# Places for the scaled q, k, v sums, and the order of the output gate's products, in a two-layer hybrid encoder

## The chip, the cores and the metric

One core of a Trainium2 chip runs the whole program. The metric is the device time of one execution in microseconds (us). The kernel before takes 1235.73 us, the median of three runs (1235.57 to 1237.52).

## What is computed

The reference is an encoder of two layers over 256 positions of width 1024, all in float32. Each layer adds half a SwiGLU block (inner width 2816), then a mixer, then half of another SwiGLU block; a norm stands ahead of each. The change lies in the mixer:

```
gq, gk, gv, gz, gb, ga, c_q, c_kv, k_rope, gate_logits = split_cols(h @ w_in[l])
qkv = silu(conv5(concat(gq, gk, gv)))        # depthwise, centred, 5 taps over the positions
qh, kh = l2norm of the 4 heads of q and of k;  vh = the 4 heads of v
o = gated delta rule forwards + backwards (chunks of 64, with a triangular solve)
y_a = (rmsnorm(o) * silu(gz)) @ gdn_proj     # gz: the output gate
y_b = 8 heads of softmax attention from the latents c_q, c_kv @ mla_proj
x = x + (sigmoid(g_A) * y_a + sigmoid(g_B) * y_b) @ w_out
```

q, k and v are 512 columns wide each, so the convolution has 1536 channels.

## The kernel before

**Products.** Every product is made of three: the activations and the weights are both split into a high part in the type fp32r and the rest, and high x high, high x low and low x high are added in PSUM. `weights` (L118) loads a block of weights with a DMA on SP's queue into `raw`, copies it on ScalarE into `whi` (L130) and subtracts on VectorE into `wlo` (L131). `mm3` issues the three products (L148 to L150). `dense_t` runs over the inner dimension for two accumulators, one per half of the 256 positions, and calls an evacuation for each. The accumulators `acc` are three PSUM tiles; two more rings are `ms` (3) and `gd` (2).

**The mixer.** The projection with `w_in` is done in pieces. `qkv_group(grp)` (L546) makes 256 of the 1536 channels, with the channels on the partitions: groups 0 and 1 are q, 2 and 3 are k, 4 and 5 are v. Its 48 products (L557) fill one `acc` tile. VectorE scales that by the norm's factor of each position into `pre` (L565), a tile of 2 x 260 elements per partition whose two elements at either end GpSimd sets to zero (L563, L564). Then, for each of the two halves of the channels, five taps are added up in `cv` on VectorE, the first as a product (L571) and four as multiply-add (L573). ScalarE makes `th`, the tanh of `cv` (L577), and VectorE finishes SiLU into `qkT` or, for v, into a part of `ysb` (L578). `pre`, `cv` and `th` have one place each, so every group waits for the one before it, and `lengths` (L581), which sums the squares of four heads (GpSimd L586, then TensorE L590), uses `cv` as well.

Other steps that are met below: `mla_dense` (L618) makes q, k and v of four attention heads from the latents, with the weights `mla_w_ukv` and then `mla_w_uq`; `mla_heads` (L642) transposes q and k of these heads on TensorE (L651), copies them out on ScalarE (L654), and returns the attention of the heads, which is run later. `gdn_decay` (L734) makes the decay matrices with products on GpSimd (L743, L755). `gdn_la` (L758) multiplies q and k (TensorE L763, VectorE L767). `gdn_base` (L780) inverts triangular blocks of 16 in fifteen serial steps on GpSimd (L805, L807) with VectorE before and after (L810), and `inv0` (L835) and the following put the blocks together on TensorE (L839 and on). `gate` (L985) makes the merge gates into tiles of the tag `gate`, which has six places. `ev_z` (L980) evacuates the output gate.

**What sets the order.** The program is written as one sequence, L1007 to L1081, and built under a planner (L1114): each instruction has a place in the sequence as its priority, and the planner runs a simulated clock and gives each engine, whenever it is free, the ready instruction that comes first. `tc.high_priority(offset=n)` lets instructions rank as if they stood n places earlier. The order that comes out is fixed: on the chip each engine works through its own queue in that order and stands still when the instruction at its head must wait. A tile can be taken only when a place of its tag is free. The part of the sequence around the change is

```
qkv_group(2); the beta, decay and q-latent columns; qkv_group(3); qkv_group(0); the kv-latent columns
gdn_scalars(); gdn_decay(0); lengths(4); latent(cq); qkv_group(1); gdn_decay(1); latent(ckv)
gdn_coeffs(); gdn_la(1); gdn_la(0); m0 = mla_dense(0); at0 = mla_heads(*m0)
gdn_base() at priority; dense(..., C_Z, ...), the output gate; inv_zero(); inv0(0) and on
mla_dense(1); two merge gates; ...; qkv_group(4); qkv_group(5); ...
```

Of the kernel before, what the change touches and what calls it, by code (L numbers as in the profile page):

```python
# [16 lines left out]
ALU = mybir.AluOpType  # L17
# [3 lines left out]
P = 128  # L21
D = 1024
S = 256
NT = 2
NKC = D // P
# [8 lines left out]
C_Z, C_BA, C_KV, C_G = 1536, 2048, 2448, 2736  # L34
# [3 lines left out]
def encoder_trunk(ctx: ExitStack, tc: tile.TileContext, x, positions, norm_ffn1, ffn1_w_gate, ffn1_w_up,  # L38
# [4 lines left out]
    V, A, G, T = nc.vector, nc.scalar, nc.gpsimd, nc.tensor  # L43
# [57 lines left out]
    xh = pitched(main, NKC, "xh")  # L101
    xl = pitched(main, NKC, "xl")
# [71 lines left out]
    def dense(ah, al, nk, src, c0, w, evac, **kw):  # L174
        dense_t([(ah[:, k], al[:, k]) for k in range(nk)], src, c0, w, evac, **kw)
# [249 lines left out]
    def mixer(l, next_gain):  # L425
# [3 lines left out]
        wl_ = w_in[l]  # L429
# [3 lines left out]
        with tc.tile_pool(name="mix", bufs=1) as mp:  # L433
            def t2(tag, bufs, shape=(P, NH, P)):
                return mp.tile(list(shape), F32, tag=tag, name=tag, bufs=bufs)
# [17 lines left out]
            rb = mp.tile([P, S], F32, name="rb")  # L453
# [92 lines left out]
            def qkv_group(grp):  # L546

                ps = acc()
                pc = ps.rearrange("p (c s) -> p c s", c=2)
                ws = weights(wl_[:, grp * 256:(grp + 1) * 256], NKC, 256)  # L550

                for c in range(2):
                    cc = slice(c * P, (c + 1) * P)
                    terms = [m for kc, (wh, wlo) in enumerate(ws)
                             for m in ((wh, xh[:, kc]), (wh, xl[:, kc]), (wlo, xh[:, kc]))]
                    for i, (w, a) in enumerate(terms[::-1] if c else terms):
                        T.matmul(pc[:, c].rearrange("p (t s) -> p t s", s=P), lhsT=w[:, cc], rhs=a, start=(i == 0),  # L557
                                 stop=(i == len(terms) - 1))
                if grp >= 4:
                    vT[grp - 4] = ysb[0][:, (grp - 4) * 512:(grp - 3) * 512].rearrange("p (c s) -> p c s", s=S)  # L560
                pre = t2("pre", 1, (P, 2, S + 4))
                cv = t2("cv", 1, (P, 2, S))
                G.memset(pre[:, :, 0:2], 0.0)  # L563
                G.memset(pre[:, :, S + 2:S + 4], 0.0)  # L564
                V.tensor_tensor(out=pre[:, :, 2:S + 2], in0=pc, in1=rb[:, None, :].to_broadcast([P, 2, S]), op=ALU.mult)  # L565
                for c in range(2):
                    ch = grp * 2 + c
                    for d in range(5):
                        wc = ccol[:, l * 60 + d * 12 + ch:l * 60 + d * 12 + ch + 1]
                        if d == 0:  # L570
                            V.tensor_scalar(out=cv[:, c], in0=pre[:, c, 0:S], scalar1=wc, scalar2=None, op0=ALU.mult)  # L571
                        else:
                            V.scalar_tensor_tensor(out=cv[:, c], in0=pre[:, c, d:d + S], scalar=wc, in1=cv[:, c],  # L573
                                                   op0=ALU.mult, op1=ALU.add)

                th = t2("th", 1, (P, 2, S))
                A.activation(out=th, in_=cv, func=AF.Tanh, scale=0.5)  # L577
                V.scalar_tensor_tensor(out=qkT[:, grp * 2:grp * 2 + 2, :] if grp < 4 else vT[grp - 4], in0=th, scalar=1.0,  # L578
                                       in1=cv, op0=ALU.add, op1=ALU.mult)

            def lengths(c0):  # L581

                pss = gdp()[:, :4 * NT * 32].rearrange("p (c t s) -> p c t s", c=4, t=NT)
                for c in (0, 2):
                    sq = t2("cv", 1, (P, 2, S))
                    G.tensor_tensor(out=sq, in0=qkT[:, c0 + c:c0 + c + 2, :], in1=qkT[:, c0 + c:c0 + c + 2, :], op=ALU.mult)  # L586
                    sv = sq.rearrange("p c (t g s) -> p g c t s", t=NT, g=4)
                    for g in range(4):

                        T.matmul(pss[g * 32:(g + 1) * 32, c:c + 2], lhsT=ones, rhs=sv[:, g], start=True, stop=True)  # L590
                rows = t2("rows", 1, (P, 2, 4 * NT * 32))
                A.copy(out=rows[:, 0], in_=pss.rearrange("p c t s -> p (c t s)"))
                V.transpose(out=rows[:, 1], in_=rows[:, 0])
                V.tensor_scalar(out=ssq[:, :, c0:c0 + 4],
                                in0=rows[:, 1].rearrange("p (c t s) -> p t c s", c=4, t=NT)[:, :, :, 0],
                                scalar1=4.0 * EPS, scalar2=None, op0=ALU.add)
                for t in range(NT):
                    G.tensor_tensor(out=rqk[:, t, c0:c0 + 4], in0=ssq[:, t, c0:c0 + 4], in1=neghalf[:, :4], op=ALU.pow)
# [422 lines left out]
            gdn_la(1)  # L1021
            gdn_la(0)
            m0 = mla_dense(0)
            at0 = mla_heads(*m0)
            with tc.high_priority(offset=2000):
                gdn_base()
            dense(xh, xl, NKC, wl_, C_Z, 512, ev_z)
            inv_zero()
            with tc.high_priority(offset=2000):
                inv0(0)  # L1030
# [88 lines left out]
```

## Time and profile before

| what | value |
|---|---|
| runs, median (lowest to highest) | 1235.73 us (1235.57 to 1237.52) |
| the profiled execution, its time | 1238.92 us |
| the profiled execution, its span | 1237.2 us |
| mean granted TensorE clock | 0.985 of full speed |
| TensorE busy | 1204.2 us, 97% |
| VectorE busy | 770.9 us, 62% |
| ScalarE busy | 622.4 us, 50% |
| GpSimd busy | 132.3 us, 11% |
| mean DMA rate | 164 GB/s |

The span is from the first to the last instruction; the execution's time has 1.72 us more. In the profile PE is TensorE's products, PEld its weight loads, DVE is VectorE, ACT ScalarE, POOL GpSimd, SP the queue that issues the DMAs of the weights. L12 is line 12 of the kernel. An instruction is written as its line, its operation, what it writes and reads by the program's tile names, and its shape; x4 says that a line stands for four instructions in a row. In square brackets is the time for which the engine had been idle before it, and the work that ended that idle time. The granted clock (PEclk) is TensorE's, as a share of 2.4 GHz: 1.00 is that, 0.50 is 1.2 GHz, and a value between them is a stretch with some of both. The two mixers lie at 196 to 432 us and at 807 to 1043 us.

### The profile page before, as it was taken

How to read it: one execution, taken by the hardware profiler on the slowest of the kernel's cores; microseconds unless marked ns; L12 is line 12 of the kernel's file. 1: busy time of each engine (PE TensorE's matmuls, PEld its weight loads, DVE VectorE, ACT ScalarE, POOL GpSimd, SP SyncE). 2: the span in 40 equal slices, each digit the busy share in tenths (PEclk: the TensorE clock that was granted, in tenths of full speed). 3: DMA queues.
4: the chain of work that ended last, by engine and by line, in shares of the span. 5: the costliest groups of instructions: out<-in, count | busy, mean ns of one | idle time of the engine just before them, and what ended most of it. 6: DMA issues, size and time to landing. Idle time of an engine off the chain costs nothing.

```text
span 1237.2 us, 17605 instructions
## 1 busy us (share of the span) xinstructions
PE 1204.2 (97%) x7064; PEld 1016.9 (82%) x7064; DVE 770.9 (62%) x1125; ACT 622.4 (50%) x911; POOL 132.3 (11%) x238
## 2 busy tenths in 40 slices
PE   9999999899999999999999999997999999999997
PEld 6888889778778888888888888897778888888886
DVE  5665556986857665554555554588858676555554
ACT  6554445547455454444454453465455455544443
POOL 1000001454101000000000000015540000000010
PEclk9999999989899999999999999998998999999999
DMA  7564555445222555556555556553453135565552
GB/s 265 181 197 144 201 188 179 139 125 174 94 88 103 171 185 189 176 173 207 187 178 187 186 170 194 182 158 122 124 168 104 69 138 186 178 198 180 191 187 85
DMA packets 114576, 202.70 MB, mean 164 GB/s; under 512 B 4107, under 2 KB 30399, under 8 KB 114495
## 3 DMA queue, kind: packets, MB, share of 16 engines
q1 hardware_dynamic: 114031, 200.52, 49.9%
q8 instruction: 55, 0.90, 0.3%
q10 hardware_dynamic: 464, 1.06, 0.2%
q14 instruction: 26, 0.21, 0.1%
HBM read 200.52 MB, written 1.05 MB: 163 GB/s over the span
## 4 chain that ended last, share of the span: by engine, by line
PE 87%; DVE 5%; POOL 4%; ACT 2%; issue 2%; DMA 0%; POOLq 0%; SPq 0%; ACTq 0%
PE acc L148 24%; PE acc L149 24%; PE acc L150 24%; PE acc L557 4%; PE ms L198 2%; DVE wlo L131 2%; POOL t L807 1%; PE ms L665 1%; POOL bt L805 1%; PE gd L148 1%; PE gd L149 1%; PE gd L150 1%; PE gd L938 1%; DVE cv L573 1%; PE gd L763 1%
## 5 line engine op out<-in xcount | busy, mean ns | idle before, releaser
L131 DVE TENSOR_TENSOR wlo<-raw,whi 128x1024 fp32r<-128x1024 f32 (+3 forms) x388 | 470.4, 1215 | 368.4 <-ACT whi L130 365.9
L130 ACT CAST whi<-raw 128x1024 fp32r<-128x1024 f32 (+3 forms) x388 | 399.3, 1033 | 424.0 <-PE acc L150 384.1
L149 PE MATMUL acc<-wlo,xh 128*128 128x512 f32 (+3 forms) x968 | 360.6, 374 | 0.0
L150 PE MATMUL acc<-whi,xl 128*128 128x512 f32 (+3 forms) x968 | 357.4, 372 | 0.0
L148 PE MATMUL acc<-whi,xh 128*128 128x512 f32 (+3 forms) x968 | 344.8, 376 | 0.1
L149 PEld LDWEIGHTS acc<-wlo,xh 128*128 128x128 f32 x968 | 182.4, 188 | 29.5 <-issue 0.4
L148 PEld LDWEIGHTS acc<-whi,xh 128*128 128x128 f32 x968 | 181.5, 189 | 30.3 <-ACT xh L115 0.8
L150 PEld LDWEIGHTS acc<-whi,xl 128*128 128x128 f32 x968 | 182.1, 188 | 29.3
L149 PE MATMUL acc<-wlo,hh 128*128 128x512 f32 x352 | 137.4, 390 | 0.0
L150 PE MATMUL acc<-whi,hl 128*128 128x512 f32 x352 | 137.1, 390 | 0.0
L148 PE MATMUL acc<-whi,hh 128*128 128x512 f32 x352 | 127.3, 392 | 0.0
L150 PEld LDWEIGHTS acc<-whi,hl 128*128 128x128 f32 x352 | 66.1, 188 | 13.8
L148 PEld LDWEIGHTS acc<-whi,hh 128*128 128x128 f32 x352 | 66.1, 188 | 13.7
L149 PEld LDWEIGHTS acc<-wlo,hh 128*128 128x128 f32 x352 | 66.1, 188 | 13.3
L148 PE MATMUL acc<-whi,fr 128*128 128x512 f32 (+1 forms) x152 | 60.3, 403 | 9.1 <-DVE pre L565 7.9
L149 PE MATMUL acc<-wlo,fr 128*128 128x512 f32 (+1 forms) x152 | 59.9, 396 | 0.0
L150 PE MATMUL acc<-whi,fr 128*128 128x512 f32 (+1 forms) x152 | 57.5, 395 | 2.4 <-DVE fr L116 2.4
L557 PE MATMUL acc<-xl,whi 128*128 128x256 f32 x192 | 55.3, 288 | 0.0
L557 PE MATMUL acc<-xh,wlo 128*128 128x256 f32 x192 | 54.2, 292 | 1.0 <-DVE wlo L131 1.0
L557 PE MATMUL acc<-xh,whi 128*128 128x256 f32 x192 | 54.9, 289 | 0.0
L573 DVE SCALAR_TENSOR_TENSOR cv<-pre,ccol,cv 128x256 f32<-128x256 f32 x96 | 51.5, 569 | 0.1
L563 POOL MEMSET pre<- 128x4 f32 x12 | 1.2, 104 | 425.3 <-PE acc L150 341.0
(298 smaller groups left out, 1271.9 us busy)
## 6 DMA issues: line engine op xcount, KB each, us to landing
raw<-in_ffn_w_up_dram SPq DMA_DIRECT2D x40, 1024.0 KB, 5.1
raw<-in_ffn_w_down_dram SPq DMA_DIRECT2D x40, 1024.0 KB, 4.9
raw<-in_ffn_w_gate_dram SPq DMA_DIRECT2D x38, 1024.0 KB, 5.0
raw<-in_w_in_dram SPq DMA_DIRECT2D x32, 1024.0 KB, 5.0
raw<-in_w_out_dram SPq DMA_DIRECT2D x8, 1024.0 KB, 4.9
raw<-in_ffn_w_gate_dram SPq DMA_DIRECT2D x12, 512.0 KB, 3.7
raw<-in_ffn_w_up_dram SPq DMA_DIRECT2D x8, 512.0 KB, 3.7
raw<-in_ffn_w_down_dram SPq DMA_DIRECT2D x8, 512.0 KB, 3.3
```

The lines of the kernel that those rows point to most:

```text
L130: A.copy(out=hi[:, :n * w], in_=raw[:, k0 * w:(k0 + n) * w])
L131: V.tensor_tensor(out=lo[:, :n * w], in0=raw[:, k0 * w:(k0 + n) * w], in1=hi[:, :n * w].bitcast(F32), op=ALU.subtract)
L148: T.matmul(ps[t][:, :n], lhsT=a1, rhs=w[0], start=start, stop=False)
L149: T.matmul(ps[t][:, :n], lhsT=a1, rhs=w[1], start=False, stop=False)
L150: T.matmul(ps[t][:, :n], lhsT=a2, rhs=w[0], start=False, stop=stop)
L198: T.transpose(out=pt[:, i * S + t * P:i * S + (t + 1) * P], in_=srcs[t][:, (j + i) * P:(j + i + 1) * P], identity=ident)
L557: T.matmul(pc[:, c].rearrange("p (t s) -> p t s", s=P), lhsT=w[:, cc], rhs=a, start=(i == 0), stop=(i == len(terms) - 1))
L573: V.scalar_tensor_tensor(out=cv[:, c], in0=pre[:, c, d:d + S], scalar=wc, in1=cv[:, c], op0=ALU.mult, op1=ALU.add)
L665: T.matmul(sc[:, t * S:(t + 1) * S], lhsT=qT[:, t * P:(t + 1) * P], rhs=kT, start=True, stop=True)
L763: T.matmul(pa[:, (h - hp) * 256:(h - hp + 1) * 256], lhsT=qkT[:, 4 + h, t * P:(t + 1) * P], rhs=qkT[:, h:h + 5:4, t * P:(t + 1) * P], star ...
L805: G.tensor_tensor(out=tv, in0=M[:, b + 1:16, b:b + 1].to_broadcast([P, na, nb]), in1=Y[:, b:b + 1, 0:nb].to_broadcast([P, na, nb]), op=ALU ...
L807: G.tensor_tensor(out=Y[:, b + 1:16, 0:nb], in0=Y[:, b + 1:16, 0:nb], in1=tv, op=ALU.add)
```

## The change

In `qkv_group`, the scaled sums of groups 0 to 3 are put into the tag `gate` (six places, before used by the merge gates alone), and `pre` remains for groups 4 and 5, without the zeroed ends: the memsets are gone, and each tap at an edge covers fewer positions, with the centre tap first. `cv` has two places instead of one. The scaling gets a priority of 150 places. The tanh is written over the scaled sums, and the tag `th` is gone. In the mixer's sequence, the output gate's products are moved ahead of `mla_heads` of the first four heads, which holds the transposes.

```diff
@@ -558,22 +558,23 @@
                                  stop=(i == len(terms) - 1))
                 if grp >= 4:
                     vT[grp - 4] = ysb[0][:, (grp - 4) * 512:(grp - 3) * 512].rearrange("p (c s) -> p c s", s=S)
-                pre = t2("pre", 1, (P, 2, S + 4))
-                cv = t2("cv", 1, (P, 2, S))
-                G.memset(pre[:, :, 0:2], 0.0)
-                G.memset(pre[:, :, S + 2:S + 4], 0.0)
-                V.tensor_tensor(out=pre[:, :, 2:S + 2], in0=pc, in1=rb[:, None, :].to_broadcast([P, 2, S]), op=ALU.mult)
+
+                pre = t2("gate", 6, (P, 2, S)) if grp < 4 else t2("pre", 1, (P, 2, S))
+                cv = t2("cv", 2, (P, 2, S))
+                with tc.high_priority(offset=150):
+                    V.tensor_tensor(out=pre, in0=pc, in1=rb[:, None, :].to_broadcast([P, 2, S]), op=ALU.mult)
                 for c in range(2):
                     ch = grp * 2 + c
-                    for d in range(5):
+                    for d in (2, 0, 1, 3, 4):
                         wc = ccol[:, l * 60 + d * 12 + ch:l * 60 + d * 12 + ch + 1]
-                        if d == 0:
-                            V.tensor_scalar(out=cv[:, c], in0=pre[:, c, 0:S], scalar1=wc, scalar2=None, op0=ALU.mult)
+                        if d == 2:
+                            V.tensor_scalar(out=cv[:, c], in0=pre[:, c], scalar1=wc, scalar2=None, op0=ALU.mult)
                         else:
-                            V.scalar_tensor_tensor(out=cv[:, c], in0=pre[:, c, d:d + S], scalar=wc, in1=cv[:, c],
+                            o, i = (slice(2 - d, S), slice(0, S + d - 2)) if d < 2 else (slice(0, S + 2 - d), slice(d - 2, S))
+                            V.scalar_tensor_tensor(out=cv[:, c, o], in0=pre[:, c, i], scalar=wc, in1=cv[:, c, o],
                                                    op0=ALU.mult, op1=ALU.add)
 
-                th = t2("th", 1, (P, 2, S))
+                th = pre
                 A.activation(out=th, in_=cv, func=AF.Tanh, scale=0.5)
                 V.scalar_tensor_tensor(out=qkT[:, grp * 2:grp * 2 + 2, :] if grp < 4 else vT[grp - 4], in0=th, scalar=1.0,
                                        in1=cv, op0=ALU.add, op1=ALU.mult)
@@ -582,7 +583,7 @@
 
                 pss = gdp()[:, :4 * NT * 32].rearrange("p (c t s) -> p c t s", c=4, t=NT)
                 for c in (0, 2):
-                    sq = t2("cv", 1, (P, 2, S))
+                    sq = t2("cv", 2, (P, 2, S))
                     G.tensor_tensor(out=sq, in0=qkT[:, c0 + c:c0 + c + 2, :], in1=qkT[:, c0 + c:c0 + c + 2, :], op=ALU.mult)
                     sv = sq.rearrange("p c (t g s) -> p g c t s", t=NT, g=4)
                     for g in range(4):
@@ -1021,10 +1022,10 @@
             gdn_la(1)
             gdn_la(0)
             m0 = mla_dense(0)
+            dense(xh, xl, NKC, wl_, C_Z, 512, ev_z)
             at0 = mla_heads(*m0)
             with tc.high_priority(offset=2000):
                 gdn_base()
-            dense(xh, xl, NKC, wl_, C_Z, 512, ev_z)
             inv_zero()
             with tc.high_priority(offset=2000):
                 inv0(0)
```

## Rows read from the trace of the kernel before

**Rows 1.** The page: the span, and busy time of each engine with its share.

```profile
span 1237.2 us, 17605 instructions
...
PE 1204.2 (97%) x7064; PEld 1016.9 (82%) x7064; DVE 770.9 (62%) x1125; ACT 622.4 (50%) x911; POOL 132.3 (11%) x238
```

**Rows 2.** Stretches of 10 us: stretch, its length, busy time of each engine, PEclk, DMA.

```profile
220.00:230.00 10.00, 10.00 (x81) 10.00 (x80) 9.32 (x26) 6.05 (x10) 0.14 (x2) 1.00 0.57 167
230.00:240.00 10.00, 8.90 (x67) 8.24 (x66) 9.88 (x16) 5.64 (x14) 8.16 (x7) 1.00 0.58 186
240.00:250.00 10.00, 4.86 (x18) 3.77 (x17) 10.00 (x14) 4.12 (x9) 6.23 (x8) 0.77 0.36 130
```

**Rows 3.** TensorE's waits over the whole span: total us, times, longest us.

```profile
PE acc L148 <- DVE pre L565: 7.9, 2, 3.9
...
PE gd L839 <- DVE XC L816: 3.4, 2, 1.7
...
PE ms L651 <- ACT qk L654: 2.8, 2, 1.4
```

**Rows 4.** Timeline of TensorE: start us, us, instruction, idle before and its releaser.

```profile
224.38 0.28 PE L557 MATMUL acc<-xh,whi 128*128 128x256 f32 x1
...
239.41 0.28 PE L557 MATMUL acc<-xh,whi 128*128 128x256 f32 x1
...
247.87 0.66 PE L148 MATMUL acc<-whi,fr 128*128 128x384 f32 x1 [3.94 <-DVE pre L565]
...
266.37 1.47 PE L651 MATMUL ms<-ident,m 128*96 128x128 f32 x12
...
268.38 0.40 PE L150 MATMUL acc<-whi,xl 128*128 128x512 f32 x1
...
271.57 0.64 PE L651 MATMUL ms<-ident,m 128*96 128x128 f32 x4 [1.40 <-ACT qk L654]
...
272.42 1.78 PE L763 MATMUL gd<-qkT 128*128 128x256 f32 x4 [0.21 <-DVE qkT L578]
...
317.29 1.07 PE L839 MATMUL gd<-XC,LA 32*32 32x32 f32 x64 [1.71 <-DVE XC L816]
...
318.94 1.09 PE L682 MATMUL ms<-ident,pr 128*128 128x128 f32 x4 [0.58 <-DVE pr L677]
```

**Rows 5.** Three stretches after TensorE's gaps, columns as in rows 2.

```profile
247.90:254.00 6.10, 6.10 (x28) 5.59 (x29) 2.72 (x5) 2.84 (x5) 1.04 (x1) 0.64 0.26 86
272.40:278.00 5.60, 5.58 (x18) 4.55 (x19) 5.60 (x14) 1.92 (x5) 0.00 (x0) 0.70 0.34 89
317.30:325.00 7.70, 7.12 (x117) 6.31 (x120) 7.17 (x15) 3.06 (x7) 0.00 (x0) 0.57 0.39 132
```

**Rows 6.** Timeline of VectorE in the convolutions of groups 0 and 1.

```profile
229.96 0.68 DVE L565 TENSOR_TENSOR pre<-acc,rb 128x512 f32<-128x512 f32 x1
...
243.85 2.01 DVE L131 TENSOR_TENSOR wlo<-raw,whi 128x768 fp32r<-128x768 f32 x1
...
247.04 0.68 DVE L565 TENSOR_TENSOR pre<-acc,rb 128x512 f32<-128x512 f32 x1
```

**Rows 7.** VectorE's instructions on tile cv alone: stretch, length, busy (count), PEclk, DMA.

```profile
205.00:215.00 10.00, 4.02 (x10) 1.00 0.62 185
233.00:247.00 14.00, 8.52 (x10) 0.94 0.46 151
```

**Rows 8.** Timeline of ScalarE about the first attention heads' copies.

```profile
269.84 0.63 ACT L577 ACTIVATE th<-cv 128x512 f32<-128x512 f32 x1 [4.93 <-DVE cv L573]
...
270.94 1.54 ACT L654 COPY qk<-ms 96x512 f32<-96x512 f32 x3
```

**Rows 9.** Timeline of GpSimd: the squares of the k heads.

```profile
248.40 1.04 POOL L586 TENSOR_TENSOR cv<-qkT 128x512 f32<-128x512 f32 x1 [1.55 <-DVE qkT L578]
...
254.02 2.01 POOL L586 TENSOR_TENSOR cv<-qkT 128x512 f32<-128x512 f32 x1 [4.58 <-PE gd L590]
```

**Rows 10.** Timeline of VectorE at the end of the serial inverse.

```profile
312.24 1.18 DVE L810 TENSOR_SCALAR g<-t,half 128x256 f32<-128x256 f32 x2 [6.62 <-POOL t L807]
```

## The prediction, made before the change was run

> **What bounds the kernel.** I read the page first, then TensorE's waits, then a table of stretches over the first mixer, then the timelines of the stretches where TensorE stood still. TensorE is busy 1204.2 of 1237.2 us [rows 1], so 33 us of standing still is nearly all that reordering can win, plus what a lower clock costs behind each gap. The gaps sit in the mixers. TensorE's longest waits each occur twice, once per layer, with equal lengths [rows 3], so I work out one mixer and double it.
>
> In the first mixer three places matter. I call them A, B and C.
>
> **A** is the first product with the q-latent weights at 247.87 us, after a gap of 3.94 us put down to `pre` L565 [rows 4]. The accumulator it needs was filled by group 1, whose last product started at 239.41 [rows 4]; VectorE scaled it out only at 247.04 [rows 6]. After the gap the granted clock over 6.10 us was 0.64, that is partly 1.2 and partly 2.4 GHz, with TensorE busy throughout [rows 5]. What 6.10 us at 0.64 lacks is 6.10 x 0.36 = 2.2 us. A costs 3.94 + 2.2 = 6.1 us.
>
> **B** is the last four of the first heads' transposes at 271.57, after 1.40 us, and 0.21 us before the next product [rows 4]. The three PSUM tiles of the earlier transposes were not copied until 270.94, because ScalarE's queue stood at the tanh of group 1 until 269.84, 4.93 us of waiting for VectorE's convolution [rows 8]. Afterwards 5.60 us ran at 0.70, which lacks 1.7 us [rows 5]. B costs 3.3 us.
>
> **C** is the first step of the block inverse, 1.71 us, and a transpose of attention, 0.58 us [rows 4]. Then 7.70 us ran at 0.57, lacking 3.3 us [rows 5]. C costs 5.6 us.
>
> VectorE bounds A from behind: it is busy 9.32, 9.88 and 10.00 of three successive 10 us [rows 2]. This is a queue in fixed order that is late, not an idle engine held by a semaphore. That is why I don't book A as won whole.
>
> **The change, part by part.**
>
> *Separate places for the scaled sums.* Groups 0 to 3 now take their tile from the six `gate` places. Group 0's last product started at 224.38 but its scaling ran at 229.96, since the only `pre` was still read by group 3's taps; group 1's ran at 247.04 [rows 4, 6]. With places of their own and 150 positions of priority, both scalings can follow their products. Group 1's costs the same 0.68 us, now ahead of the low half of the q-latent weights, which ran 243.85 to 245.86 [rows 6]. It then ends at 246.54 and the product need not wait until 247.87: 1.33 us won. The six places are enough for the gates, whose first tile is wanted long after these groups; I cost that at nothing.
>
> *Two `cv` tiles.* The ten taps of one group took 4.02 us in the stretch 205 to 215 and 8.52 us in 233 to 247 [rows 7]. In the second of these GpSimd is busy with the decay products, 8.16 and 6.23 of 10 us, against 0.14 in 220 to 230 [rows 2]. With a second `cv`, group 0 can start before 230, but VectorE has only 10 - 9.32 = 0.68 us free there [rows 2]. Taps that fill 0.68 us there save 0.68 x 8.52 / 4.02 = 1.4 us behind it. So A gives 1.33 + 1.4 = 2.7 us. The bounds of A are 6.1 us won, if the queue falls so that the weights come first, and a loss that the slower rival prices. I take 2.7, near the low end, because the saturated rows are the nearest.
>
> The second `cv` also frees GpSimd: the second square of the k heads waited 4.58 us for the sum over the first, since both used the one tile [rows 9]. And group 1's convolution no longer waits behind those squares, so its tanh should not hold ScalarE at B. I book B whole, 3.3 us; its bounds are 0 and 3.3.
>
> *Twelve pairs of memsets fall away on GpSimd, and the taps at the edges are 1 or 2 elements shorter of 256.* Not on TensorE's path: nothing. `th` written into `pre` costs groups 0 to 3 nothing. Only groups 4 and 5 still share one `pre`, and there group 5's scaling must now wait for group 4's last product with tanh too; this part is hidden by the gate products, and costs at most one 0.68 us scaling [rows 6] if that cover is gone.
>
> *The output gate's products first.* The order is by readiness, and these products already ran before B: twelve transposes got in at 266.37, and the last gate product started at 268.38 [rows 4]. So the move exchanges some 2 us of work within TensorE's queue without adding or removing any. Its weights' transfers and halves move with it on SP, ScalarE and VectorE, by the same 2 us, past the heads' four copies. I take nothing; bounds 1.40 us either way, the size of the gap at B.
>
> *C.* Its chain starts from group 1's convolution and the k lengths, which should both come earlier, by about what TensorE gains. VectorE then stands 6.62 us behind GpSimd's serial inverse [rows 10], which nothing here shortens. I leave C as it is; bounds: 5.6 won, or the 2.7 + 3.3 = 6.0 of A and B given back.
>
> **Sum.** 2.7 + 3.3 = 6.0 us per mixer, 12 us in all. The profiled execution took 1238.92 us (1.72 us around its span), so it becomes 1226.9; the median of the runs is 3.19 us lower than that execution, which gives 1223.7.
>
> A rule that speaks against this: in rows 7 the same ten instructions take twice as long where GpSimd is busy. The Trainium skill, in "SBUF — State Buffer", section "Who interferes with whom", calls the shared port pair an exclusive lock between VectorE and GpSimd, not a split of bandwidth; by that rule, which these rows agree with, the two squares moved from 248.40 and 254.02 into VectorE's fullest stretch would each stop it for their whole length. At 1.04 us each [rows 9] that would take 2.1 us off A, and the sum would be 3.9 us per mixer, 1227.9.
>
> **The rivals.**
>
> *Both gaps go whole.* If the weights' halves stand ahead of the taps in VectorE's queue, A gives 6.1 and B 3.3: 18.8 us in two mixers, 1216.9. For it: TensorE needs little from VectorE then, and taps can wait. Against it: 10.00 of 10 us [rows 2]. If C went too, another 11.2: 1205.7.
>
> *Given back at C.* TensorE comes to the inverse 6.0 us earlier; if the chain through GpSimd does not, the gap at C grows by as much, and the time stays 1235.7. For it: C is a gap already, and VectorE stands behind GpSimd there [rows 10]. Against it: the chain's start is freed by the same second tile [rows 9].
>
> *Slower: taps in front of weights.* Group 1's taps used to be held back by the one `cv` until the q-latent weights were through. Freed, and earlier in program order than those weights, they can enter VectorE's queue ahead of them at A. The low half would then end at 246.54 plus ten taps, 4.02 to 8.52 us [rows 7]; at the middle, 6.3, that is 252.8, 4.9 us after the old 247.87. B's 3.3 us come back, so each mixer loses 1.6 us and the time is 1239. It decides from 247.87 + 3.3 - 246.54 = 4.6 us of taps in that place.
>
> *The move of the gate products does nothing*, since the order is by readiness: that is in the sum already.
>
> **How the numbers follow.** What a measurement of this kernel can tell from no change is about 0.2%, 2.5 us. I give the forecast (A in part, B whole, by the rule or without) 0.50, both gaps whole 0.17, given back 0.15, slower 0.18. Faster: 0.50 + 0.17 = 0.67. Same: 0.15, of which 0.02 go to slower, since what is given back need not be exact: 0.13. Slower: 0.20. The range must hold 8 in 10: it runs from both gaps whole with half of C, 1216.9 - 5.6 = 1211.3, rounded to 1211, to the middle of the slower case, 1239.
>
> **What would show it.** Right: `pre` of groups 0 and 1 starts within 2 us of their last products; group 1's taps lie before 257; ScalarE no longer waits 4.9 us at that tanh; the 1.40 us gap at B is gone and the granted clock behind it is 1.0; the gap at A is between 0.5 and 2.5 us; TensorE's instruction count is unchanged. Wrong: a gap at A of over 4 us with taps of group 1 before the q-latent low half (the slower rival); a gap at C of 6 us or more (given back); or new waits of TensorE in stretches where it had none.

## The result, and the profile after

| | before | after |
|---|---|---|
| runs, median (lowest to highest) | 1236.62 us (1235.57 to 1239.12) | 1227.95 us (1227.65 to 1230.41) |
| the profiled execution, its time | 1238.92 us | 1228.15 us |
| mean granted TensorE clock | 0.985 | 0.996 |
| VectorE busy | 770.9 us | 775.8 us |
| GpSimd busy | 132.3 us | 135.5 us |

The ratio of after to before is 0.9929, with a 95% interval from 0.9910 to 0.9948: the kernel is faster by 0.7%. The direction held. The forecast was 1223.7 us, 4.3 us below the median measured; by the medians the gain is 8.7 us, where 12.0 were forecast.

The head of the page after answers to [rows 1].

```profile
span 1226.4 us, 17565 instructions
...
PE 1194.4 (97%) x7064; PEld 1009.1 (82%) x7064; DVE 775.8 (63%) x1125; ACT 622.8 (51%) x911; POOL 135.5 (11%) x214
```

TensorE issues the same 7064 products and is busy 9.8 us less (1204.2 before). Of the 10.8 us that the span lost, only 1 us was standing still (33.0 to 32.0). By TensorE's own ledger, then, the change removed little idle time; it removed busy time, for the same products. Two things limit this reading. Before's profiled execution lies 2.3 us above its median and after's 0.2 us, so some 2 of the 10.8 us lie between executions and not between the kernels. And where another engine is the late one, idle time and busy time at a lower clock can take each other's place (last section): the ledger says where the time went, not why. What stands behind it is read from VectorE further down.

To see where, I cut out the two mixers, from the first transpose of the norm ahead of each (L198) to the first of the norm behind it. Stretches of the kernel before, then of after: stretch, its length, busy time of each engine (TensorE, its weight loads, VectorE, ScalarE, GpSimd, with the count of instructions), PEclk, DMA.

```profile
197.88:431.23 233.35, 221.37 (x1705) 190.38 (x1704) 176.81 (x331) 127.41 (x231) 58.19 (x91) 0.96 0.41 132
808.87:1042.19 233.32, 221.38 (x1705) 190.39 (x1704) 176.85 (x331) 127.50 (x231) 58.12 (x91) 0.96 0.41 132
```

```profile
197.82:425.22 227.40, 216.75 (x1705) 186.71 (x1704) 178.86 (x331) 127.68 (x231) 59.77 (x81) 0.99 0.42 136
802.85:1031.12 228.27, 216.94 (x1705) 186.80 (x1704) 179.51 (x331) 127.66 (x231) 59.78 (x81) 0.99 0.42 135
```

Both mixers issue 1705 products before and after. The first is 5.95 us shorter, the second 5.05, and the SwiGLU blocks between them take 377.64 and 377.63 us. So all of it lies in the mixers. In the first, 4.62 us of the 5.95 is busy time and 1.33 is idle time. In the second it is 4.44 and 0.61. By the granted clock of these rows the first mixer lacked some 233.35 x 0.04 = 9 us before and 227.40 x 0.01 = 2 us after, busy and idle time together, so the clock can account for all the busy time that went.

TensorE's waits after, which answer to [rows 3]: total us over both layers, times, longest us.

```profile
PE gd L840 <- DVE XC L817: 4.9, 2, 2.4
PE acc L150 <- DVE fr L116: 4.0, 4, 1.7
PE acc L149 <- DVE wlo L131: 2.9, 6, 0.5
PE gd L764 <- DVE LA L768: 2.8, 2, 1.4
PE acc L148 <- ACT m L626: 2.5, 2, 1.2
```

The two waits for `pre` and for the copies `qk` at the heads' transposes are gone from the list. In their place stand shorter ones: for the low halves of weights, for `LA`, for `m`. The timeline of TensorE after shows the same places, against [rows 4].

```profile
243.80 0.73 PE L150 MATMUL acc<-whi,fr 128*128 128x512 f32 x2 [1.67 <-DVE fr L116]
244.40 0.44 PE L148 MATMUL acc<-whi,fr 128*128 128x384 f32 x1
...
246.64 0.44 PE L149 MATMUL acc<-wlo,fr 128*128 128x384 f32 x1 [0.40 <-DVE wlo L131]
...
267.54 1.10 PE L764 MATMUL gd<-qkT 128*128 128x256 f32 x4 [1.40 <-DVE LA L768]
...
278.14 0.50 PE L148 MATMUL acc<-whi,xh 128*128 128x512 f32 x1 [1.24 <-ACT m L626]
...
306.84 0.75 PE L840 MATMUL gd<-XC,LA 32*32 32x32 f32 x64 [2.44 <-DVE XC L817]
```

At A the first q-latent product (128x384) starts at 244.40 instead of 247.87, without a gap of its own. B has a gap of the same length, 1.40 us, but put down to `LA`, and a second one of 1.24 us behind it. C is one gap of 2.44 us instead of 1.71 and 0.58, at 306.84 instead of 317.29. That is 10.5 us earlier, though the mixer ends only 6 us earlier: less of the other work had been run by then (599 products from the start of the mixer, against 646).

Three stretches behind these places, of the lengths of [rows 5]. The first is where A's products stood in the kernel before; behind after's own first one, from 244.40 to 250.50, the clock is 1.00 as well.

```profile
247.90:254.00 6.10, 5.55 (x32) 4.08 (x31) 6.10 (x7) 3.72 (x7) 6.10 (x8) 1.00 0.23 81
267.40:273.00 5.60, 5.46 (x27) 4.73 (x28) 5.60 (x13) 2.39 (x5) 0.00 (x0) 1.00 0.18 53
306.80:314.50 7.70, 7.66 (x220) 7.15 (x221) 4.13 (x10) 3.78 (x10) 0.27 (x1) 0.78 0.42 140
```

The granted clock is 1.00, 1.00 and 0.78 where it was 0.64, 0.70 and 0.57. VectorE's busy time in 10 us stretches, the third of the five, answers to [rows 2]:

```profile
220.00:230.00 10.00, 10.00 (x82) 10.00 (x81) 10.00 (x29) 6.04 (x10) 0.00 (x0) 1.00 0.53 164
230.00:240.00 10.00, 8.85 (x66) 7.94 (x64) 10.00 (x15) 5.48 (x13) 8.10 (x6) 1.00 0.55 167
240.00:250.00 10.00, 7.82 (x49) 6.01 (x50) 10.00 (x14) 6.59 (x13) 8.04 (x8) 1.00 0.43 152
```

VectorE is still the engine that is late, now at 10.00 of 10 in each. From the first to the second stretch its instructions fall from 29 to 15, as GpSimd goes from 0.00 to 8.10 us busy (their shapes differ too; like instructions are compared further down). Over 230 to 272, A and B together, before and then after:

```profile
230.00:272.00 42.00, 34.35 (x191) 28.61 (x189) 36.08 (x57) 19.45 (x38) 29.73 (x33) 0.92 0.43 139
```

```profile
230.00:272.00 42.00, 36.20 (x205) 29.73 (x204) 41.10 (x64) 21.82 (x43) 31.13 (x29) 1.00 0.42 140
```

VectorE was busy 36.08 of 42 us before and 41.10 after. These 5 us in which it no longer stands still are about what a mixer gained, but not all of them are more work done: over the whole first mixer its same 331 instructions took 2.05 us longer (178.86 for 176.81). Two lines of its timeline before show where it stood, behind A:

```profile
253.91 1.23 DVE L131 TENSOR_TENSOR wlo<-raw,whi 128x1024 fp32r<-128x1024 f32 x1 [3.38 <-ACT whi L130]
...
257.99 0.66 DVE L571 TENSOR_SCALAR cv<-pre,ccol 128x256 f32<-128x256 f32 x2 [0.87 <-PE gd L590]
```

It waited for ScalarE's copy of a weight block, which in turn waited for TensorE's products at the lower clock (the copy at 252.82 had stood 1.12 us for the last product L150), and then for the one `cv`, which held the squares until TensorE's L590 products had read them. The taps of group 1, which could have filled these waits, had no place. After, they do fill them. The sums themselves, on VectorE's timeline, answer to [rows 6]:

```profile
224.81 0.68 DVE L565 TENSOR_TENSOR gate<-acc,rb 128x512 f32<-128x512 f32 x1
...
241.56 1.79 DVE L131 TENSOR_TENSOR wlo<-raw,whi 128x768 fp32r<-128x768 f32 x1
...
243.67 0.67 DVE L565 TENSOR_TENSOR gate<-acc,rb 128x512 f32<-128x512 f32 x1
...
247.29 1.39 DVE L571 TENSOR_SCALAR cv<-gate,ccol 128x256 f32<-128x256 f32 x2
```

Group 0 is scaled at 224.81 (229.96 before) and group 1 at 243.67 (247.04). Group 1's taps begin at 247.29. The tanh of group 1 on ScalarE, against [rows 8], and the squares of the k heads on GpSimd, against [rows 9]:

```profile
259.60 0.63 ACT L578 ACTIVATE gate<-cv 128x512 f32<-128x512 f32 x1 [4.99 <-DVE cv L574]
```

```profile
232.88 2.04 POOL L587 TENSOR_TENSOR cv<-qkT 128x512 f32<-128x512 f32 x1 [0.96 <-DVE gl L113]
...
247.44 1.08 POOL L587 TENSOR_TENSOR cv<-qkT 128x512 f32<-128x512 f32 x1
```

### The profile page after: what moved, and what is told of

Its sections match the earlier page's. It is cut to its first block, busy times and chain, and to the rows that moved or that the text cites. A ratio compares the mean times of both kernels' runs of the same rounds, so it can differ in the third digit from the quotient of the medians.

```text
span 1226.4 us, 17565 instructions
## 1 busy us (share of the span) xinstructions
PE 1194.4 (97%) x7064; PEld 1009.1 (82%) x7064; DVE 775.8 (63%) x1125; ACT 622.8 (51%) x911; POOL 135.5 (11%) x214
## 4 chain that ended last, share of the span: by engine, by line
PE 82%; DVE 11%; POOL 2%; issue 2%; ACT 2%; DMA 0%; POOLq 0%; SPq 0%; ACTq 0%; DVEq 0%
PE acc L148 23%; PE acc L149 23%; PE acc L150 23%; DVE wlo L131 4%; PE acc L557 3%; DVE cv L574 2%; PE ms L198 2%; POOL t L808 1%; POOL bt L806 1%; PE ms L666 1%; DVE LA L768 1%; PE gd L149 1%; PE gd L148 1%; PE gd L150 1%; PE gd L957 1%
## 5 line engine op out<-in xcount | busy, mean ns | idle before, releaser
L150 PE MATMUL acc<-whi,xl 128*128 128x512 f32 (+3 forms) x968 | 357.2, 372 | 0.0
L148 PE MATMUL acc<-whi,xh 128*128 128x512 f32 (+3 forms) x968 | 346.0, 376 | 2.6 <-ACT m L626 2.5
L148 PEld LDWEIGHTS acc<-whi,xh 128*128 128x128 f32 x968 | 181.4, 188 | 34.1 <-ACT m L626 3.3
L150 PEld LDWEIGHTS acc<-whi,xl 128*128 128x128 f32 x968 | 182.1, 188 | 29.3
L150 PE MATMUL acc<-whi,hl 128*128 128x512 f32 x352 | 137.1, 389 | 0.0
L148 PE MATMUL acc<-whi,hh 128*128 128x512 f32 x352 | 127.4, 392 | 0.0
L150 PEld LDWEIGHTS acc<-whi,hl 128*128 128x128 f32 x352 | 66.1, 188 | 13.7
L148 PEld LDWEIGHTS acc<-whi,hh 128*128 128x128 f32 x352 | 66.1, 188 | 13.7
L150 PE MATMUL acc<-whi,fr 128*128 128x512 f32 (+1 forms) x152 | 56.5, 387 | 4.0 <-DVE fr L116 4.0
L148 PE MATMUL acc<-whi,fr 128*128 128x512 f32 (+1 forms) x152 | 58.9, 396 | 1.3 <-ACT fr L112 1.3
L262 ACT ACTIVATE sil<-acc,rstd 128x512 f32<-128x512 f32 (+1 forms) x48 | 31.0, 654 | 29.6 <-PE acc L150 29.5
L834 POOL MEMSET Z<- 128x1024 f32 x4 | 3.7, 962 | 341.1 <-PE acc L150 341.1
```

The source lines that it names most:

```text
L148: T.matmul(ps[t][:, :n], lhsT=a1, rhs=w[0], start=start, stop=False)
L150: T.matmul(ps[t][:, :n], lhsT=a2, rhs=w[0], start=False, stop=stop)
L262: A.activation(out=sil[t][:, :w], in_=ps, func=AF.Silu, scale=rstds[0][:, t:t + 1])
```

## The experiments

All twelve were timed in five rounds, in three batches of four, each batch on one chip with the kernel before beside it (1237.25, 1236.95 and 1237.96 us). Ratios are to it, with their 95% intervals; the kernel after is compared by its own ratio, 0.9929. Where an edit adds lines, the line numbers behind it are shifted.

**The move alone** (before, with only the gate products moved):

```diff
             m0 = mla_dense(0)
+            dense(xh, xl, NKC, wl_, C_Z, 512, ev_z)
             at0 = mla_heads(*m0)
             with tc.high_priority(offset=2000):
                 gdn_base()
-            dense(xh, xl, NKC, wl_, C_Z, 512, ev_z)
```

> The kernel before with the output gate's products moved ahead of the first heads' transposes, and nothing else. Theory 'places' (the separate places keep TensorE's clock up, the move does nothing): within 2.5 us of the kernel before, and TensorE's 3.94 us gap at the q-latent products with a granted clock of about 0.64 behind it is still there. Theory 'move' (the moved products fill the gap at the heads' copies and so carry the gain): 4 us or more faster than before, and the 1.40 us gap is gone.

It took 1239.58 us, ratio 1.0016 [1.0004, 1.0028]: no gain, but a loss of about 2 us (0.5 to 3.5 by the interval). The wait for the copies at B left the list of waits, and another took its place at the next product:

```profile
PE acc L148 <- DVE pre L565: 7.9, 2, 3.9
PE gd L763 <- DVE qkT L578: 4.5, 2, 2.2
```

Before, B was 1.40 us for the copies and then 0.21 us for `qkT`; with the move it is 2.2 us for `qkT`. TensorE was waiting for group 1's convolution in both, by two roads.

**The places alone** (after, with the move undone, the same diff the other way round):

> The changed kernel with the output gate's products put back behind the transposes. 'Places': within 2.5 us of the changed kernel, 1225.5 to 1230.5, clock near 1.00 behind the gaps at the q-latent products. 'Move': back to 1234 to 1237.

1230.06 us, ratio 0.9944 [0.9931, 0.9957]. The places carry the gain. What the move adds on top, 0.9929 against 0.9944, lies inside the intervals and stays unresolved. The clock behind the q-latent products was expected near 1.00; from 240 to 250 it was 0.83. In this run the gap at L764 is 0.52 us and the one at L148 behind it 2.38 us, against 1.40 and 1.24 in after: the move exchanges one gap for another here too.

**One `cv`** (after, both `cv` lines back to one place):

```diff
-                cv = t2("cv", 2, (P, 2, S))
+                cv = t2("cv", 1, (P, 2, S))
...
-                    sq = t2("cv", 2, (P, 2, S))
+                    sq = t2("cv", 1, (P, 2, S))
```

> The changed kernel with one place for cv instead of two. If the second cv is what matters (it lets a group's taps and the squares of the k heads run without waiting for the group before): 1233 to 1237, with a gap of 3 us or more before the q-latent products. If the places of the scaled sums alone matter: 1226 to 1230.

1247.78 us, ratio 1.0082 [1.0067, 1.0097]: slower than before, by more than any rival gave, and not at A, B or C. The early stretch went better than in after (220 products from 230 to 272, against 205). The loss is at the end of the mixer, where TensorE has run out of other work; its timeline there, and VectorE's:

```profile
387.80 2.62 PE L957 MATMUL gd<-LA 128*128 128x128 f32 x22
394.46 1.00 PE L493 MATMUL ms<-ident,g 128*128 128x128 f32 x2 [4.04 <-DVE g L974]
```

```profile
391.78 0.16 DVE L968 TENSOR_TENSOR s<-s,oss 128x4 f32<-128x4 f32 x1 [0.63 <-ACT junk L963]
...
394.06 1.14 DVE L974 SCALAR_TENSOR_TENSOR g<-g,fac,zsil 128x128 f32<-128x128 f32 x4
```

TensorE waits 4.04 us for the output of the delta rule, a chain of small operations (0.16 us and so on) across several engines. In before and after, products of a merge gate (L148 to L150 on `xh`) and then others on `fr` still stand in TensorE's queue at that time and run until the chain is done; they begin at 378.45 and 372.43. Here they began at 369.25 and were used up.

**One `cv` without the move** (the edit above, and the move undone), to see whether that late wait came with the move:

> The kernel of the run with one cv, and the gate products back behind the transposes. That run lost 11 us against the changed kernel although its inverse began 8.0 us earlier than before: TensorE waited 4.0 us for the gated outputs at the end of the gated DeltaNet. If that late wait comes from the one cv itself (the squares of the q heads are made late): it is here again, 1240 to 1249. If it is an accident of one planned order: the late wait is gone, and the time is 1230 to 1236.

1245.95 us, ratio 1.0065 [1.0049, 1.0080], and the same wait at L493, again 4.0 us. It comes with the one `cv`, not with the move. Why the planned order, which is made once for the whole mixer, spends those products earlier with one `cv`, I have not settled.

**One `pre`** (after, with only the second `cv` and the move):

```diff
-                pre = t2("gate", 6, (P, 2, S)) if grp < 4 else t2("pre", 1, (P, 2, S))
+                pre = t2("pre", 1, (P, 2, S))
```

> The changed kernel with one place for the scaled sums of all six groups (and for the tanh written over it), cv still two. If the places of the scaled sums matter (the scaling frees the accumulator early): 1231 to 1237, with TensorE waiting for the scaling of group 1. If cv alone matters: 1226 to 1230.

1234.41 us, ratio 0.9977 [0.9966, 0.9988]. The gap at A returned, longer than before, and so did the lower clock. The wait, the two stretches around it, and two lines of VectorE's timeline:

```profile
PE acc L148 <- DVE pre L565: 12.1, 2, 6.1
```

```profile
240.00:250.00 10.00, 4.46 (x25) 2.53 (x23) 9.83 (x14) 2.84 (x7) 9.62 (x10) 0.82 0.28 101
250.00:260.00 10.00, 8.47 (x38) 7.64 (x39) 8.61 (x15) 5.50 (x10) 4.46 (x8) 0.67 0.16 52
```

```profile
249.98 0.70 DVE L579 SCALAR_TENSOR_TENSOR qkT<-pre,cv 128x512 f32<-128x512 f32 x1 [0.17 <-ACT pre L578]
250.78 0.69 DVE L565 TENSOR_TENSOR pre<-acc,rb 128x512 f32<-128x512 f32 x1
```

This run isn't quite the kernel before with a second `cv`. The tanh is still written over the sums, so the one place is held until group 0's SiLU is finished (249.98), and group 1's scaling follows only then; in before the scaling (247.04) did not wait for that. How much of the gap of 6.1 us instead of 3.9 comes from this was not measured. Against after, this run's span is 8.3 us longer, 5.9 us of it idle time of TensorE (37.9 against 32.0): with two `cv` already there, what the places for the sums take away is mostly waiting.

With these runs the two kinds of places can be told apart, as they are built here. The second `cv` with one place for the sums is worth some 3 us (1234.41). The places for the sums with one `cv` lose 8 to 10.5 us. Both together win 7 to 9. They are not two terms that add up.

**Filling the gap at A** (before, with 14 products of no use, put behind the product that ends ahead of the gap):

```diff
+                if hf in (0,):
+                    m = state["mm"]
+                    fp = msp()
+                    for _ in range(14):
+                        with tc.issue_after(m.ins if hasattr(m, "ins") else m):
+                            m = T.matmul(fp, lhsT=junk[:, :P], rhs=junk, start=True, stop=True)
```

> The kernel before, with 14 products of no use put on TensorE between the last kv-latent product and the first q-latent product, where it stands still for 3.94 us; no wait is taken away, and the result does not use them. Theory 'clock' (most of the change's gain is that TensorE's clock no longer falls, not that it waits less): the granted clock behind that place is 1.00 instead of 0.64, the q-latent products run at 0.17 us apart instead of 0.32, and the time falls by some 2 us per mixer, to 1232 to 1234. Theory 'wait' (the length of the wait is what counts): no gain, 1236 to 1241.

In the place itself the clock went as the theory says. TensorE's timeline:

```profile
243.94 3.19 PE L639 MATMUL ms<-junk 128*128 128x512 bf16 x14
248.04 0.41 PE L148 MATMUL acc<-whi,fr 128*128 128x384 f32 x1 [0.91 <-DVE pre L565]
...
252.09 0.34 PE L150 MATMUL acc<-whi,fr 128*128 128x384 f32 x1
```

The first q-latent product starts 0.17 us later than before (247.87), and the 248.00 to 252.42 stretch runs at a clock of 1.00; the same products of before ended at 253.25, at 0.59 from 247.90 to 253.30. The total, though, was 1247.62 us, ratio 1.0080 [1.0063, 1.0097], slower than either theory gave: the inserted products changed the planned order further on, and the wait of 4.0 us at L493 stands here too, with a clock of 0.76 from 390 to 400. So the cost of the clock is shown in place, not in the total. In place it is large: from 230 to 272 this run issues 220 products, 206 without the fourteen, where before issued 191 and after 205. VectorE's wait of 3.38 us for the weight copy is 1.36 us here.

**Filling the gap at C** (after, with 16 such products of 256 columns ahead of the inverse's first step):

```diff
+                    if not oT:
+                        m = mlast[-1]
+                        with tc.high_priority(offset=4000):
+                            for _ in range(16):
+                                with tc.issue_after(m.ins if hasattr(m, "ins") else m):
+                                    m = T.matmul(po[:, S:], lhsT=junk[:, :P], rhs=junk[:, S:], start=True, stop=True)
```

> The changed kernel, with 16 products of no use on TensorE in the 2.44 us before the first step of the block inverse, where the clock still falls (0.51 and 0.64 in the 4 us behind it). 'Clock': 1.00 behind it, 1.5 us per mixer, 1224 to 1226.5. 'Wait': 1227 to 1231.

1226.67 us, ratio 0.9915 [0.9899, 0.9931]; 1.3 us below after, where 3 were expected. That lies between the two theories and inside the intervals, so the total decides neither. TensorE's timeline, and three stretches:

```profile
304.51 1.92 PE L702 MATMUL ms<-junk 128*128 128x256 bf16 x16
306.99 0.75 PE L847 MATMUL gd<-XC,LA 32*32 32x32 f32 x64 [0.56 <-DVE XC L824]
```

```profile
240.00:250.00 10.00, 8.08 (x38) 6.42 (x39) 10.00 (x14) 5.56 (x12) 8.04 (x8) 0.83 0.44 151
...
300.00:310.00 10.00, 9.44 (x126) 7.81 (x125) 4.85 (x8) 4.20 (x8) 3.74 (x13) 1.00 0.39 125
310.00:320.00 10.00, 8.64 (x270) 8.08 (x269) 7.08 (x19) 5.35 (x14) 1.50 (x4) 1.00 0.15 48
```

The gap at C is filled (in the other layer 1.4 us remain, put to issue) and the clock behind it is 1.00 (after: 0.90 and 0.93 in these two stretches). The first line is the surprise: up to the inverse this kernel has after's order of products, with the same gap of 1.67 us ahead of A, and yet its clock was 0.83 there, where after's was 1.00. The run with the places alone shows the same 0.83 behind a gap of 1.66 us.

**GpSimd's work moved to ScalarE.** The remaining question was what makes VectorE late. If it is GpSimd beside it, then taking GpSimd's work away must make VectorE's own instructions shorter. First, the squares alone (after):

```diff
-                    G.tensor_tensor(out=sq, in0=qkT[:, c0 + c:c0 + c + 2, :], in1=qkT[:, c0 + c:c0 + c + 2, :], op=ALU.mult)
+                    A.activation(out=sq, in_=qkT[:, c0 + c:c0 + c + 2, :], func=AF.Square)
```

> The changed kernel with the squares of lengths made on ScalarE instead of GpSimd. If the two squares that the change moved into VectorE's full stretch hold VectorE up: some 1 to 2 us per mixer, 1224 to 1226.5. If they cost nothing there: 1226.5 to 1230; if ScalarE's queue is held up by them instead: later than 1230.

1225.81 us, ratio 0.9905 [0.9886, 0.9923]. GpSimd's busy time fell by 13.1 us, VectorE's by 7.6 us (775.8 to 768.2) with the same 1125 instructions, the time by 2.1 us, which is inside the intervals of the two and so not resolved.

Second, the decay products alone (after), eight per mixer, each as four pieces of 128 columns with the factor as ScalarE's scale:

```diff
-                        G.tensor_tensor(out=gm, in0=hb, in1=bc(gsp[i][:, t, d * 4:d * 4 + 4].bitcast(F32)), op=ALU.mult)
+                        for h in range(NH):
+                            A.activation(out=gm[:, h, :], in_=hi_m, func=AF.Copy,
+                                         scale=gsp[i][:, t, d * 4 + h:d * 4 + h + 1].bitcast(F32))
```

> The changed kernel with the eight decay products per mixer taken from GpSimd and made on ScalarE, as 32 pieces of 128 columns. If GpSimd's work is what doubles VectorE's taps: ten taps in 4 to 5.5 us, VectorE no longer at 10.00 of 10 us from 230 to 260, and 1220 to 1226. If ScalarE becomes the late queue in its place: taps as short, but 1229 to 1240.

1221.95 us, ratio 0.9877 [0.9855, 0.9899], 6 us below after. GpSimd fell by 24.8 us, VectorE by 17.2, ScalarE rose by 17.3. The stretches of A:

```profile
230.00:240.00 10.00, 9.29 (x69) 8.61 (x68) 9.69 (x19) 9.99 (x29) 2.74 (x2) 1.00 0.73 236
240.00:250.00 10.00, 7.80 (x51) 5.93 (x49) 6.78 (x17) 10.00 (x31) 5.78 (x9) 1.00 0.25 85
```

Group 0's ten taps, in the place of those of [rows 7], took 5.30 us; in after they took 7.56. VectorE is no longer full, but ScalarE is, 9.99 and 10.00 of 10, and TensorE's gaps in this stretch (0.70, 1.17 and 0.49 us) are all put down to ScalarE. Here the bound has moved to it.

Third, the same edit on the kernel before:

> The kernel before with the decay products on ScalarE. If VectorE's queue at the q-latent products is late because GpSimd holds it up: the gap there shrinks below 2 us, ten taps of group 0 take 4 to 5.5 us instead of 8.5, 1226 to 1232. If it is late by the single places alone: the gap of 3 us or more remains, 1234 to 1239.

1234.14 us, ratio 0.9970 [0.9959, 0.9981]. Group 0's ten taps, against the 8.52 us of [rows 7]:

```profile
232.00:239.00 7.00, 4.02 (x10) 1.00 0.70 233
```

They take 4.02 us, as long as group 2's between 205 and 215. The gap of 3.9 us for `pre` is gone from the list although the sums still have one place, so GpSimd's company was part of what made A: single places make that gap only beside it. But the time is that of the other theory: the gain is 4 us, less than the places give, since another wait of 2.8 us stands there now, for ScalarE:

```profile
PE acc L148 <- ACT fr L115: 5.7, 2, 2.8
```

Fourth, both on ScalarE (after):

> The changed kernel with both the squares and the decay products on ScalarE. If GpSimd's work beside VectorE is the cost: better than either alone (1225.8 and 1222.0), 1217 to 1221. If ScalarE is full by then (it was busy 10.00 of 10 us from 240 to 250 with the decay products): 1221 to 1228.

1227.39 us, ratio 0.9915 [0.9898, 0.9933]: some 5 us worse than the decay products alone. ScalarE is full again (9.99 and 10.00 of 10), and TensorE waits 2.1 us per mixer for `fr` L115 from it. That this is the whole of the 5 us is argued and not shown: the planned order differs too.

Fifth, a balance: the squares and the half of the decay products that takes the high part of the gates on ScalarE, the low part on GpSimd. This stands ahead of the four pieces of the diff above, beside the diff of the squares:

```diff
+                        if i:
+                            G.tensor_tensor(out=gm, in0=hb, in1=bc(gsp[i][:, t, d * 4:d * 4 + 4].bitcast(F32)), op=ALU.mult)
+                            T.matmul(pe, lhsT=lo_m, rhs=gm.rearrange("p h d -> p (h d)"), start=(i == 0), stop=(i == 1))
+                            continue
```

> The changed kernel with the squares and half of the decay products (those of the high part) on ScalarE, the low part on GpSimd. If both engines limit: between the run with the decay products on ScalarE and better, 1217 to 1222. If only GpSimd's share counts: 1222 to 1225, between the two runs.

1215.39 us (1214.99 to 1216.46), ratio 0.9817 [0.9799, 0.9835], faster than either expectation gave. That beats both kernels: 22.6 us below before in its batch and, by the ratios, 1.1% below after.

```profile
230.00:240.00 10.00, 9.29 (x71) 8.62 (x71) 9.96 (x20) 9.97 (x25) 3.08 (x3) 1.00 0.59 172
240.00:250.00 10.00, 9.66 (x60) 7.25 (x58) 8.68 (x15) 9.51 (x23) 9.12 (x12) 1.00 0.44 151
```

From 230 to 262 TensorE is busy 30.95 of 32 us (after: 27.60), VectorE 29.32 (32.00) and ScalarE 24.98 (17.15). No engine is full from end to end. TensorE's longest wait in the mixers is 1.1 us, and C is a gap of 0.8 us in one layer.

## Why the prediction was right, and where not

**The direction and the carrier: right.** The places carry the gain (1230.06 with them alone, 1239.58 with the move alone), and the gap for `pre` at A comes back when the sums' places go (6.1 us). The move was booked at nothing with bounds of 1.40 us; the move alone loses 0.5 to 3.5 us by its interval, and the ratio of the places alone, 0.9944, lies inside after's interval.

**The sum per mixer: right by luck in its parts.** Booked were 6.0 us; the mixers gave 5.95 and 5.05 in the profiled executions, and 4.3 each by the medians. But 4.3 of the booked 6.0 were gaps (2.7 at A, 1.61 at B) and 1.7 the clock. Measured were 1.33 and 0.61 us of idle time, and 4.62 and 4.44 us of busy time, which goes with the clock. The terms that failed are B, "I book B whole, 3.3 us", whose gap stayed, and A, whose 2.2 us of lower clock the 2.7 left out.

*A.* The product starts 3.47 us earlier against 2.7 booked, but not as I had put it. Group 1's scaling did not follow its products (the last of them starts at 238.34); it still ran behind the low half of 128x768, 0.32 us after that ended at 243.35. What came earlier was that half itself, 241.56 for 243.85. VectorE filled the 0.68 us that it had free in 220 to 230, as booked, and the queue behind got shorter by 2.3 us instead of 1.4; another 0.9 us is that two taps and the next low half, of 128x384, no longer stand between that half and the scaling. And I had not seen that the rest of the gap would come back elsewhere: from 230 to 262 TensorE's idle time fell from 6.25 to 4.40 us only, since it now waits a little for several things of the same full queue (0.40, 0.53 and 0.54 us for `wlo`, and 1.67 for `fr`, 1.21 before). The rest of A's worth was what I had left out: the clock behind it, and through the weight copies VectorE's standing still, 5 us in A and B together.

*B.* Wrong in its mechanism. ScalarE still waits 4.99 us at the tanh of group 1, so the step "should not hold ScalarE at B" failed. It just does so earlier (254.6 to 259.6 instead of 264.9 to 269.8), when no copies of the heads stand behind it. A gap as long remained, for `LA`, and another of 1.24 us joined it. The 1.7 us of clock came back as booked: 1.00 behind both.

*C.* Booked as unchanged, and as a gap it is: 2.44 for 1.71 and 0.58 us. The clock behind it, 0.78 for 0.57, lacks 7.7 x 0.22 = 1.7 us instead of 3.3. So "given back at C" did not happen. VectorE's wait behind GpSimd's inverse shrank from 6.62 to 5.11 us, against [rows 10].

```profile
303.40 1.19 DVE L811 TENSOR_SCALAR g<-t,half 128x256 f32<-128x256 f32 x2 [5.11 <-POOL t L808]
```

*The signs.* Of what was to show it right, this held: TensorE's count of products is unchanged, group 0's scaling follows its last product (224.81 after 224.32), the gap at A lies in the range named (1.67 us, now two products earlier), and the clock behind B is 1.00. This did not: group 1's scaling comes 5.3 us after its last product, its taps go on to 259.57 instead of ending before 257, ScalarE still waits 4.99 us at the tanh, and a gap of 1.40 us stands at B. One sign of being wrong came true: a new wait of 1.24 us, at 278.14.

*Slower, taps in front of weights.* It did not happen: group 1's taps begin at 247.29, after the low halves of 128x768 and 128x384 (241.56 and 244.94) and the first q-latent products. A slowdown does lie near by, but of another kind: with one `cv` it is 10 us, at the end of the mixer, which no view of before pointed to.

**From the profile to the median: this made the number wrong.** Between the two profiled executions lie 10.77 us, near the 12.0 of the sum. I then took 3.19 us off, since before's profiled execution lay that far above its median. After's profiled execution lies only 0.20 us above its own. The excess of before's was not a constant of the profiler that after would carry as well. It goes with the granted clock of that one execution, 0.985: of the 47 executions of before that were timed beside the experiments, the 20 with a clock of 0.985 or less took 1238.89 us or more, and the 27 with a higher one 1237.96 us or less. 1226.9 us, the sum without that step, is 1 us from the median measured.

*The sum with the squares taken off, 1227.9 us.* It lies 0.05 us from the median, and that is luck too: it rests on the same gaps and the same 3.19 us. Without that step it is 1231.1. Only the first of the two squares runs ahead of A's products (232.88, against 244.40), and it takes 2.04 us and not 1.04; the second follows them. The run without the squares on GpSimd won some 2.1 us in both mixers together, inside the intervals, where 4.2 were booked.

**The company of GpSimd.** The two squares did move into VectorE's fullest stretch, at 232.88 and 247.44, and the first took 2.04 us. Beside it a tap of VectorE took 1.26 us, and the next, beside a decay product, 1.09, where their like took 0.48 at 224.33. Taking such work off GpSimd gave VectorE back 7.6 of 13.1 us and 17.2 of 24.8 us, in the busy times of whole executions; in the other three runs that did so it was 19.6 of 33.9, 15.4 of 21.7 and, on the kernel before, 14.1 of 19.5 us.

The Trainium skill, "SBUF — State Buffer", section "Who interferes with whom", says that the one thing VectorE and GpSimd contend for is the pair of ports that they share, and that this is an exclusive lock. The runs agree that the company costs much, and they measure it: 0.58 to 0.72 of GpSimd's time, not the whole of it. Part of the rest may be time in which VectorE had nothing to do; that was not separated.

## What to carry to other kernels

When the engine that is late stands still for lack of a place shortly behind the wait that it causes, more places can pay even if they only break the long wait into short ones. Look then at who makes that engine slow. Moving a share of GpSimd's elementwise work to the engine with room, and no more than that one has room for (1215.39 with half, 1221.95 and 1227.39 with more of it on ScalarE), gave more than the buffers did. And measure two buffers together as well as singly: here both win 7 to 9 us, one kind wins 3 and the other loses 8 to 10.5, since a planned order can change far from the edit.

## What was not expected of the hardware

*The same gap, two clocks.* The gap of 1.67 us at 243.8 was followed by a clock of 1.00 in the profiled execution after, and the same gap by 0.83 over 240 to 250 in the run with the gap at C filled. In before, the gap of 1.40 us at B was followed by 0.70; the one of 1.40 us in after by 1.00. One kernel's executions differ too: the mean granted clock of before was 0.984 to 0.991 in the 47 above. So the length of one gap does not decide it, and a clock read in one place of one execution is weak evidence; what decides it is left open.

*A lower clock that costs next to nothing.* After and the run with the gap at C filled, which have the same order up to the inverse, start the products just ahead of it (L693, there L694) at 303.32 and 303.50. From 230 to 262 TensorE was busy 27.60 us at a clock of 1.00 in one and 28.84 us at 0.95 in the other, and VectorE 32.00 of 32 in both. Here, where VectorE is the late engine, the slower products only filled the wait; in before, where VectorE stood still behind them (3.38 us, and 1.36 with the gap at A filled), they cost.

*The priority of 150 places has no effect.* This is the planner's doing, not the chip's: built without it, the program is the same, instruction for instruction. The scaling of group 1 still starts 5.3 us after the last of its products.
